# A two-layer decoder trunk in split fp32: the order of the opening, the first transfers, the last bank, and the gate sums

## The chip, the core and the metric

The kernel runs on one core of a Trainium2 chip. The core has a matrix engine (TensorE, here PE, with PEld for its weight loads), a vector engine (DVE), an activation engine (ACT), a general engine (POOL) and a queue engine that mainly issues DMA transfers (SP). Each runs its own instructions in order and waits on the others through semaphores. Sixteen DMA engines move data between HBM and the on-chip memory. Results of matmuls land in PSUM, which has eight banks of 128 x 512 fp32 values.

The metric is the time on the device of one execution, in microseconds (us); lower is better.

## The reference, cut to what matters

The input is 256 tokens of width 2048. Two layers run in turn, each a token mixer followed by an MLP with a squared ReLU of width 8192; each reads an RMS-normed stream and adds to it.

```python
def fox_attention(h, w_in, b_f, q_gain, k_gain, w_out):
    proj = h @ w_in                                   # q | k | v | forget gates
    q = rms_norm(q, q_gain); k = rms_norm(k, k_gain)  # per head of 128
    c = jnp.cumsum(jax.nn.log_sigmoid(f + b_f), axis=1)
    s = q @ k.T * scale + c_query - c_key             # causal
    return (softmax(s) @ v) @ w_out

def dilated_attention(h, w_in, q_gain, k_gain, w_out):
    # three groups of heads, dilations 1, 4, 16, ALiBi; one shared v;
    # the groups are merged by their softmax denominators
    return (num / den) @ w_out

for i in range(2):
    x = x + mixer_i(rms_norm(x, mix_norm_g[i]))
    h = rms_norm(x, mlp_norm_g[i])
    x = x + (relu(h @ w_up) ** 2) @ w_down
```

All weights are fp32, some 446 MB with the rest of what is read, and each weight is used once.

## The kernel before

**Split products.** Every fp32 operand of a large product is cut into a high part in the format that PE multiplies in one pass and a low part with the rest, and a product is three matmuls: high by high, high by low, low by high. A weight tile has 256 rows by 512 columns (512 KB). It is loaded as `raw` (five buffers), then `split` makes `wh` with a cast on ACT (L340) and `wl` with a subtraction on DVE (L341), five buffers each. `load` issues the transfers on SP's queue (L321); a `split` also issues the load of the tile four further on.

**A product.** `product_steps` goes through the 16 chunks of 128 input channels. One chunk is a step: two halves of the tokens by three matmuls of 512 columns (L375 to L377), six matmuls. Every second step ends one weight tile and splits another. The first layer's attention runs four rounds of three products (q, k, v); the forget gates are summed between the first q product and the first k product (`gate`, L706).

**Jobs and steps.** All work beside the products is written as generators. `jobs.tick()` runs after each step; a generator that yields a number sleeps for so many steps, one that yields a key sleeps until the key is done. So the program text puts the side work into a trace order between the matmuls. A scheduler then chooses the order of each engine's queue from that trace, unless edges forbid it. `pin` adds such edges: each traced instruction is tied behind the one before it on its engine. It is switched on at step 24. Ahead of it, and in places behind it, `behind(...)` ties single instructions behind others: casts, transposes, transfers, squares.

**The opening.** Eight transposes of the identity (`wake`, L146) run first. x comes in four tiles of 512 channels: `load_x(0)` issues the first one, half on SP and half on ACT's queue, then the first weight tile in the same way. The gain rows of the norm come on POOL's queue (`g_mix`, L158) and are turned on PE (L165). All later loads are held back by a one-element clear on DVE (L304) that is tied behind the copy of the turned gains (L166). `norm_chain` turns x for the first norm in eight pieces: four 128-column transposes into one bank (L518), scaled into a high part on ACT (L523) and a low part on DVE (L524). `more_constants` loads gate weights (`wf`, L191), gate bias and further gains after nine steps. The sums of squares (L534) run later, and the norm's factor is applied behind the first products.

**The end and the second layer's attention.** `last_product` is the last of the four products of the last MLP; it goes through three parts (tokens 0 to 127 whole, tokens 128 to 255 in two halves of 256 columns) with a bank for each, all three from the pool `ps_acc` of four banks, and each part is added up and stored as soon as it is done (L899, L901). The product before it holds two of the four banks until DVE has added them (L886). `dil_head` computes a head of the second layer: scores, softmax, a transposition through DRAM (`p_turned`), a split of the probabilities (`p_split`, ACT L669 and DVE L672), and after three more steps (two for the last pair of heads) the products with v (`pv`, L642 and L643, tile `po_d`).

Of the kernel before, what the change touches and what calls it, by code (L numbers as in the profile page):

```python
# [43 lines left out]
class Jobs:  # L44
# [5 lines left out]
    def __init__(self):  # L50
        self.now = 0
        self.live = []
        self.done = set()
        self.running = False
        self.each_step = lambda: None
# [37 lines left out]
def trunk(ctx: ExitStack, tc, x, fox_w_in, fox_b_f, fox_q_gain, fox_k_gain, fox_w_out, dil_w_in,  # L93
# [3 lines left out]
    pinned = {"last": None}  # L97
# [6 lines left out]
    def pin():  # L104
# [5 lines left out]
        if pinned["last"] is None:  # L110
            at = len(traced)
# [22 lines left out]
    nc.gpsimd.memset(warm, 0.0)  # L134
    nc.scalar.activation(warm, warm, AF.Exp)
# [6 lines left out]
    spare = ps_sc.tile([P, P], F32, tag="sc", name="spare")  # L142

    def wake(times):
        for _ in range(times):
            nc.tensor.transpose(spare, ident, ident)  # L146

    wake(8)
# [5 lines left out]
    def gain_rows(name, sources, queue=nc.sync):  # L154
        rows = work.tile([2 * KC, P], F32, tag="s", name=name, bufs=S_BUFS)
        at = 0
        for src in sources:
            queue.dma_start(rows[at:at + src.shape[0], :], src)  # L158
            at += src.shape[0]
        return rows[0:at, :]  # L160

    def gain_columns(name, rows, at):
# [3 lines left out]
        return nc.vector.tensor_copy(gain[:, at:at + n], ps[:, :n])  # L166

    per_chunk = "l (c p) -> (l c) p"
    mix_rows = gain_rows("g_mix", [mix_norm_g.rearrange(per_chunk, p=P)], nc.gpsimd)
# [17 lines left out]
    def more_constants():  # L187
        yield 9
        wf = work.tile([P, KC, FH], F32, tag="t2", name="wf")
        with behind(issued["load"]):  # L190
            nc.sync.dma_start(wf, fox_w_in[0][:, 3 * D:3 * D + FH].rearrange("(c p) n -> p c n", p=P))  # L191
            nc.sync.dma_start(bf, fox_b_f.to_broadcast([P, FH]))
            qk_rows = gain_rows("g_qk", [fox_q_gain, fox_k_gain, dil_q_gain[0], dil_k_gain[0]])
            mlp_rows = gain_rows("g_mlp", [mlp_norm_g.rearrange(per_chunk, p=P)])
        di = distances()
        yield 6
        with behind(*issued["n0"]):
            nc.scalar.copy(wfs[:, :, 0:FH], wf)
            nc.vector.tensor_sub(wfs[:, :, FH:2 * FH], wf, wfs[:, :, 0:FH].bitcast(F32))
# [88 lines left out]
    def behind(*instructions):  # L288
        stack = ExitStack()
        for i in instructions:  # L290
            stack.enter_context(tc.issue_after(getattr(i, "ins", i)))
        return stack

    def move(dst, src):

        with behind(issued["load"]):
            return nc.sync.dma_start(dst, src)
# [12 lines left out]
    def load():  # L310
# [6 lines left out]
        for c, width in cols:  # L317
            src = w[r:r + RAW_SUB * P, c:c + width].rearrange("(c p) n -> p c n", p=P)
            if i:
                with hold(t[:, 0, 0:1]):  # L320
                    issued["load"] = nc.sync.dma_start(t[:, :, at:at + width], src)  # L321
            else:

                for part, queue in enumerate((nc.sync, nc.scalar)):
                    queue.dma_start(t[:, part, at:at + width], src[:, part, :])
# [4 lines left out]
    def split():  # L330
        i = state["split"]
        per = RAW_SUB // W_SUB
        if i >= len(plan) * per:
            return
        raw = raws[i // per][:, (i % per) * W_SUB:(i % per + 1) * W_SUB, :]
        hi = wpool.tile([P, W_SUB, NC], F32R, tag="wh", name=f"wh{i}", bufs=W_BUFS)
        lo = wpool.tile([P, W_SUB, NC], F32R, tag="wl", name=f"wl{i}", bufs=W_BUFS)
        with behind(*([issued["gained"]] if i == 0 else issued.get("n0", []) if i < 2 * W_BUFS else [])):
            for part in ([slice(0, 1), slice(1, 2)] if i < 1 else [slice(0, W_SUB)]):
# [656 lines left out]
    with behind(issued["transposed"]):  # L996
        wake(3)
# [67 lines left out]
```

## Time and profile before

| | us |
|---|---|
| median of three runs | 2149.95 |
| lowest and highest run | 2149.67, 2149.97 |
| the profiled execution, its own time | 2150.94 |
| the profiled execution, span from first to last instruction | 2149.2 |
| PE busy in it | 2136.6 |
| DVE busy | 1425.8 |
| ACT busy | 1094.9 |
| POOL busy | 42.3 |

A row of the timeline has the start in us, the length in us, the engine, the line, the operation, the tile that is written `<-` those read, the shapes, and how many instructions are merged; in brackets the idle time of the engine before it and what ended it. PE's matmuls are pipelined: the row of one is longer than its share of the stream, so the pitch is read from start to start. A row of a stretch has its ends, its length, then busy time and number of instructions for PE, PEld, DVE, ACT and POOL (or for PE alone), the granted clock, the share of the DMA engines' time and GB/s. A row of waits has total time, number and the longest. "SPq" and "ACTq" are instructions that issue transfers.

### The profile page before, as it was taken

What the parts mean: (1) busy time and instruction counts of PE and PEld (TensorE: products, weight loads), DVE (VectorE), ACT (ScalarE), POOL (GpSimd) and SP (SyncE); (2) the same over time, 40 slices, a digit from 0 to 9 for tenths busy, and PEclk for the clock granted to TensorE, in tenths of its full rate; (3) what the DMA queues carried; (4) which work ended last, traced back from release to release, by engine and by line L of the source; (5) the groups of instructions that cost most, each with busy time, mean ns of one, the idle gap of its engine ahead of it and who ended that gap; (6) DMA issues with size and microseconds to landing.
All of it is one profiled execution on the core that took longest, in us unless ns stands there. A gap on an engine that the chain in (4) does not pass through costs nothing.

```text
span 2149.2 us, 29907 instructions
## 1 busy us (share of the span) xinstructions
PE 2136.6 (99%) x11120; PEld 1906.8 (89%) x11120; DVE 1425.8 (66%) x1893; ACT 1094.9 (51%) x1521; POOL 42.3 (2%) x40
## 2 busy tenths in 40 slices
PE   9999999999999999999999999999999999999998
PEld 7888888988998998998888888889988988988988
DVE  6788876785665565566668787667655655665664
ACT  6565655643443454455555655646544444444442
POOL 0000000000000000000010010000000000000000
PEclk9999999999999999999999999999999999999999
DMA  7888877766666656657777777768666566666663
GB/s 240 254 260 270 253 244 237 231 219 205 187 216 204 198 201 206 201 189 254 243 241 231 245 238 217 254 201 273 207 204 201 189 216 201 193 210 203 202 210 136
DMA packets 314531, 471.97 MB, mean 220 GB/s; under 512 B 36424, under 2 KB 124048, under 8 KB 314384
## 3 DMA queue, kind: packets, MB, share of 16 engines
q1 hardware_dynamic: 313792, 469.38, 68.2%
q8 instruction: 87, 1.43, 0.3%
q10 hardware_dynamic: 560, 0.66, 0.1%
q14 instruction: 60, 0.49, 0.1%
q0 software_dynamic: 32, 0.02, 0.0%
HBM read 446.35 MB, written 23.62 MB: 219 GB/s over the span
## 4 chain that ended last, share of the span: by engine, by line
PE 97%; DVE 1%; ACT 1%; DMA 1%; issue 0%; SPq 0%; POOL 0%; ACTq 0%; DVEq 0%; POOLq 0%
PE acc L375 21%; PE acc L376 21%; PE acc L377 21%; PE up_n1a_acc L440 5%; PE up_n3a_acc L440 5%; PE up_n3a_sc L440 3%; PE up_n1a_tp L440 3%; PE up_n1a_sc L440 3%; PE up_n3a_tp L440 3%; PE up_n1a_acc L444 3%; PE up_n3a_acc L444 3%; PE up_n3a_sc L444 1%; PE up_n3a_tp L444 1%; PE up_n1a_sc L444 1%; PE up_n1a_tp L444 1%; DVE wl L341 0%
## 5 line engine op out<-in xcount | busy, mean ns | idle before, releaser
L341 DVE TENSOR_TENSOR wl<-raw,wh 128x1024 fp32r<-128x1024 f32 (+1 forms) x801 | 970.1, 1221 | 636.9 <-ACT wh L340 624.7
L340 ACT CAST wh<-raw 128x1024 fp32r<-128x1024 f32 (+1 forms) x801 | 830.6, 1047 | 880.3 <-PE acc L377 580.0
L375 PE MATMUL acc<-wh,hT_n 128*128 128x512 f32 x896 | 343.1, 384 | 0.1
L376 PE MATMUL acc<-wl,hT_n 128*128 128x512 f32 x896 | 340.5, 380 | 0.1
L377 PE MATMUL acc<-wh,hT_n 128*128 128x512 f32 x896 | 340.3, 380 | 0.0
L376 PE MATMUL acc<-wl,aTh_n1a 128*128 128x512 f32 x512 | 194.2, 379 | 0.0
L377 PE MATMUL acc<-wh,aTl_n1a 128*128 128x512 f32 x512 | 194.2, 379 | 0.0
L375 PE MATMUL acc<-wh,aTh_n1a 128*128 128x512 f32 x512 | 194.2, 379 | 0.0
L377 PEld LDWEIGHTS acc<-wh,hT_n 128*128 128x128 f32 x896 | 169.9, 190 | 23.8
L375 PEld LDWEIGHTS acc<-wh,hT_n 128*128 128x128 f32 x896 | 170.0, 190 | 22.9 <-ACT wh L340 0.5
L376 PEld LDWEIGHTS acc<-wl,hT_n 128*128 128x128 f32 x896 | 170.2, 190 | 22.5 <-DVE wl L341 0.4
L376 PE MATMUL acc<-wl,aTh_n3a 128*128 128x512 f32 x480 | 182.1, 379 | 0.0
L377 PE MATMUL acc<-wh,aTl_n3a 128*128 128x512 f32 x480 | 182.1, 379 | 0.0
L375 PE MATMUL acc<-wh,aTh_n3a 128*128 128x512 f32 x480 | 182.1, 379 | 0.0
L440 PE MATMUL up_n1a_acc<-hT_n,wh 128*128 128x512 f32 x512 | 181.7, 382 | 0.0
L440 PE MATMUL up_n3a_acc<-hT_n,wh 128*128 128x512 f32 x512 | 181.6, 382 | 0.0
L444 PE MATMUL up_n3a_acc<-hT_n,wl 128*128 128x256 f32 x512 | 139.6, 273 | 0.0
L444 PE MATMUL up_n1a_acc<-hT_n,wl 128*128 128x256 f32 x512 | 139.6, 273 | 0.0
L376 PEld LDWEIGHTS acc<-wl,aTh_n1a 128*128 128x128 f32 x512 | 96.9, 189 | 13.7
L377 PEld LDWEIGHTS acc<-wh,aTl_n1a 128*128 128x128 f32 x512 | 96.9, 189 | 13.6
L440 PEld LDWEIGHTS up_n3a_acc<-hT_n,wh 128*128 128x128 f32 x512 | 97.0, 189 | 13.4
L375 PEld LDWEIGHTS acc<-wh,aTh_n1a 128*128 128x128 f32 x512 | 96.9, 189 | 13.4
(673 smaller groups left out, 3158.2 us busy)
## 6 DMA issues: line engine op xcount, KB each, us to landing
raw<-in_mlp_w_up_dram SPq DMA_DIRECT2D x256, 512.0 KB, 4.5
raw<-in_mlp_w_down_dram SPq DMA_DIRECT2D x256, 512.0 KB, 4.5
raw<-in_dil_w_in_dram SPq DMA_DIRECT2D x192, 256.0 KB, 3.3
raw<-in_fox_w_in_dram SPq DMA_DIRECT2D x95, 512.0 KB, 4.9
raw<-in_fox_w_out_dram SPq DMA_DIRECT2D x32, 512.0 KB, 4.5
raw<-in_dil_w_in_dram SPq DMA_DIRECT2D x32, 512.0 KB, 4.2
raw<-in_dil_w_out_dram SPq DMA_DIRECT2D x32, 512.0 KB, 3.8
blocks_n<-turned_n SPq DMA_DIRECT2D x96, 64.0 KB, 2.1
```

The source lines that it names most:

```text
L340: issued["cast"] = nc.scalar.copy(hi[:, part, :], raw[:, part, :])
L341: issued["cut"] = nc.vector.tensor_sub(lo[:, part, :], raw[:, part, :], hi[:, part, :].bitcast(F32))
L375: nc.tensor.matmul(acc[t], ah[:, tok], hi, start=first, stop=False)
L376: nc.tensor.matmul(acc[t], ah[:, tok], lo, start=False, stop=False)
L377: issued["product"] = nc.tensor.matmul(acc[t], al[:, tok], hi, start=False, stop=last)
L440: issued["product"] = nc.tensor.matmul(banks[b], hi[:, i, col], in_turn(tokens.rearrange("p x s -> p (x s)"), P // 2), start=first, stop=last)
L444: nc.tensor.matmul(banks[b][:, 0:S], lo[:, i, col], in_turn(tokens[:, 0, :], P // 2), start=False, stop=False)
```

## The change

- `pin` starts with the first instruction and is run at each step, and every `behind(...)` is taken out. The queues of all engines then follow the trace from the start.
- `wake` becomes a matmul of 512 columns with zeros that DVE clears, six ahead of everything and one behind the turned gains, in a bank of `ps_acc`.
- The first tile of x comes in three pieces (128, 128 and 256 channels), the gains behind the first of them, all on SP's queue; the first weight tile in two row blocks, the first on ACT's queue, the second on SP's. The seven loads behind the second weight tile are held back by a clear of the whole tile on POOL.
- The first three weight tiles are split by row blocks, and up to step 27 splits are placed by hand (`opening`) instead of one at each second step.
- The transposes of the first norm write each 256-column piece into a bank of its own (`ps_tp` and `ps_sc`) and come at other steps: x's tiles at 0, 3, 5 and 9 instead of 0, 2, 6 and 10, with two steps between the halves of the last two tiles. The squares of the first norm come a little later.
- `more_constants` issues its transfers after five steps instead of nine, and splits the gate weights one step earlier.
- `gate` sums high and low parts in one matmul of 512 columns, 16 instead of 32; DVE adds the two halves afterwards.
- `dil_head` waits four steps instead of three ahead of `pv` (but for the last pair).
- `last_product` takes its third bank from `ps_tp`.

```diff
-    nc.gpsimd.memset(warm, 0.0)
-    nc.scalar.activation(warm, warm, AF.Exp)
+    pinned["last"] = nc.gpsimd.memset(warm, 0.0).ins
+    jobs.each_step = pin
...
-    spare = ps_sc.tile([P, P], F32, tag="sc", name="spare")
+    spare = ps_acc.tile([P, NC], F32, tag="acc", name="spare")
+    zeros = work.tile([P, NC], F32R, tag="w", name="zeros", bufs=6)
+    nc.vector.memset(zeros.bitcast(F32), 0.0)
     def wake(times):
         for _ in range(times):
-            nc.tensor.transpose(spare, ident, ident)
-    wake(8)
+            nc.tensor.matmul(spare, zeros[:, 0:P], zeros, start=True, stop=True)
+    wake(6)
...
     def more_constants():
-        yield 9
+        yield 5
         wf = work.tile([P, KC, FH], F32, tag="t2", name="wf")
-        with behind(issued["load"]):
-            nc.sync.dma_start(wf, fox_w_in[0][:, 3 * D:3 * D + FH].rearrange("(c p) n -> p c n", p=P))
+        nc.sync.dma_start(wf, fox_w_in[0][:, 3 * D:3 * D + FH].rearrange("(c p) n -> p c n", p=P))
...
-        yield 6
-        with behind(*issued["n0"]):
-            nc.scalar.copy(wfs[:, :, 0:FH], wf)
+        yield 9
+        nc.scalar.copy(wfs[:, :, 0:FH], wf)
...
-    def hold(first):
-        if "held" not in issued:
-            return ExitStack()
-        with behind(issued["gained"]):
-            nc.vector.memset(first, 0.0)
-        return behind(*([issued["load"]] if issued["held"] == [] else []))
+    def hold(whole):
+        if "paced" in issued:
+            nc.gpsimd.memset(whole, 0.0)
...
+    def split_part(i, part):
+        raw, (hi, lo) = raws[i], splits[i]
+        nc.scalar.copy(hi[:, part, :], raw[:, part, :])
+        nc.vector.tensor_sub(lo[:, part, :], raw[:, part, :], hi[:, part, :].bitcast(F32))
...
             if i == W_SUB - 1:
                 used[0] += 1
-                split()
+                if "opening" not in issued:
+                    split()
...
-        acc = [ps_acc.tile([P, NC], F32, tag="acc", name=f"last{x}") for x in range(len(parts))]
+        acc = sums() + [ps_tp.tile([P, NC], F32, tag="tp", name="last")]
...
-                pt = ps_tp.tile([P, 2, S], F32, tag="tp", name=f"ptx_{tag}_{pr}")
...
+                for i, (pool, of) in enumerate(((ps_tp, "tp"), (ps_sc, "sc"))):
+                    pt = pool.tile([P, S], F32, tag=of, name=f"ptx_{tag}_{pr}_{i}")
...
-                yield 1
+                yield 1 if n < 2 else 2
...
-        pf = ps_sc.tile([2 * FH, S], F32, tag="sc", name="pf")
+        pf = ps_sc.tile([2 * FH, 2 * S], F32, tag="sc", name="pf")
         for k in range(KC):
-            for x, h in enumerate(lhs_h(tag)(k)):
-                nc.tensor.matmul(pf, wfs[:, k, :], h, start=k + x == 0, stop=k + x == KC)
+            both = hT[tag][k // 2][:, k % 2]
+            nc.tensor.matmul(pf, wfs[:, k, :], both.rearrange("p x s -> p (x s)"), start=k == 0, stop=k == KC - 1)
...
-        nc.vector.tensor_copy(f, pf)
+        nc.vector.tensor_copy(f, pf[:, 0:S])
+        nc.vector.tensor_add(f, f, pf[:, S:2 * S])
...
-        yield 2 if q4 == 3 else 3
+        yield 2 if q4 == 3 else 4
...
+    load_x(0, 0, P)
+    mix_rows = gain_rows("g_mix", [mix_norm_g.rearrange(per_chunk, p=P)])
+    load_x(0, P, 2 * P)
+    nc.sync.dma_start(first_raw[:, 1, :], first_w[:, 1, :])
+    load_x(0, 2 * P, NC)
...
+    load()
+    issued["paced"] = True
+    for what in (lambda: load_x(1), load, load, lambda: load_x(2), load):
+        what()
+    gain_columns("g_mix", mix_rows, 0)
+    wake(1)
+    row_blocks = [slice(i, i + 1) for i in range(W_SUB)]
+    split(())
+    split_part(0, row_blocks[0])
+    jobs.spawn(first(0))
+    split_part(0, row_blocks[1])
+    next_load()
+    load_x(3)
+    del issued["paced"]
+    issued["opening"] = True
+
+    def opening():
+        yield 1
+        split(row_blocks)
+        yield 2
+        split(row_blocks)
+        yield 1
+        split()
+        for _ in range(5):
+            yield 2
+            split()
+        yield 1
+        del issued["opening"]
         while state["split"] - used[0] < W_BUFS:
+            yield 4
             split()
```

More of the change, by code (lines that the diff above doesn't have):

```diff
@@ L318, in load @@
             src = w[r:r + RAW_SUB * P, c:c + width].rearrange("(c p) n -> p c n", p=P)
[L319 to L325, printed above, removed]
+            hold(t)
+            nc.sync.dma_start(t[:, :, at:at + width], src)
             at += width
@@ L969, in normed @@
         return lambda n: norm_chain(tag, col, n, ssp, wait(n), later(n))
[L972 to L980 removed]
+    first = normed("n0", 0, lambda n: (0, 3, 5, 9)[n], lambda n: (13, 12, 9, 7)[n])
@@ L989, in trunk @@
-    issued["gained"] = gained
-    issued["held"] = True
-    for what in (load, lambda: load_x(1), load, lambda: load_x(2), load, lambda: load_x(3), load):
-        what()
-        issued["held"] = []
-    del issued["held"]
-    jobs.spawn(first(0))
-    with behind(issued["transposed"]):
-        wake(3)
-    split()
     for n in range(1, NX):
         jobs.spawn(first(n))
-    jobs.spawn(rest())
+    jobs.spawn(opening())
     jobs.spawn(more_constants())
```

133 lines of the change are left out of this document (52 added, 81 removed).

## The prediction

> **What bounds the kernel now.** I read the page first: the span, the busy row, the chain of waits by engine.
>
> ```profile
> span 2149.2 us, 29907 instructions
> ...
> PE 2136.6 (99%) x11120; PEld 1906.8 (89%) x11120; DVE 1425.8 (66%) x1893; ACT 1094.9 (51%) x1521; POOL 42.3 (2%) x40
> ...
> PE 97%; DVE 1%; ACT 1%; DMA 1%; issue 0%; SPq 0%; POOL 0%; ACTq 0%; DVEq 0%; POOLq 0%
> ```
>
> TensorE (PE) is the bound. The change takes little work off it, so its worth lies in the 12.6 us in which PE is not busy and in products that run at a wrong pitch. The view of PE's waits says where the idle time is.
>
> ```profile
> PE spare L146 <- POOL ident masks.py:199: 2.5, 1, 2.5
> PE last L418 <- DVE x L886: 2.2, 1, 2.2
> PE po_d L642 <- DVE pTl_d L672: 1.9, 1, 1.9
> PE ps_g_mix L165 <- DMA g_mix<-in_mix_norm_g_dram: 1.8, 1, 1.8
> ...
> PE pf L706 <- DVE wfs L199: 0.2, 1, 0.2
> ```
>
> Each of the five is touched by the change. Next the timeline of the opening (start, length, engine, line, work).
>
> ```profile
> 0.84 0.20 POOL masks.py:197 MEMSET ident<- 128x128 f32 x1
> 0.98 0.10 POOL L139 MEMSET mhalf<- 128x8 f32 x1
> ...
> 2.53 1.97 PE L146 MATMUL spare<-ident 128*128 128x128 f32 x8 [2.53 <-POOL ident masks.py:199]
> ...
> 5.84 1.14 ACT L340 CAST wh<-raw 128x512 fp32r<-128x512 f32 x2 [3.09 <-DMA raw<-in_fox_w_in_dram]
> ...
> 6.34 0.31 PE L165 MATMUL ps_g_mix<-ident,g_mix 32*128 32x32 f32 x1 [1.84 <-DMA g_mix<-in_mix_norm_g_dram]
> ...
> 6.58 1.11 PE L518 MATMUL ptx_n<-ident,x 128*128 128x128 f32 x4
> ...
> 6.91 1.40 DVE L341 TENSOR_TENSOR wl<-raw,wh 128x512 fp32r<-128x512 f32 x2
> 6.93 0.38 SPq L321 DMA_DIRECT2D raw<-in_fox_w_in_dram  x1
> ...
> 7.74 0.47 ACT L523 ACTIVATE hT_n<-ptx_n,gain 128x256 fp32r<-128x256 f32 x1 [0.76 <-DVE wl L341]
> ...
> 8.24 0.48 DVE L524 SCALAR_TENSOR_TENSOR hT_n<-ptx_n,gain,hT_n 128x256 fp32r<-128x256 f32 x1
> ...
> 8.26 0.80 PE L375 MATMUL acc<-wh,hT_n 128*128 128x512 f32 x1
> ...
> 9.28 0.64 PE L375 MATMUL acc<-wh,hT_n 128*128 128x512 f32 x1
> ...
> 9.71 0.64 PE L376 MATMUL acc<-wl,hT_n 128*128 128x512 f32 x1
> ...
> 12.20 0.38 PE L376 MATMUL acc<-wl,hT_n 128*128 128x512 f32 x1
> 12.42 0.38 PE L377 MATMUL acc<-wh,hT_n 128*128 128x512 f32 x1
> ...
> 34.59 0.38 PE L377 MATMUL acc<-wh,hT_n 128*128 128x512 f32 x1
> ```
>
> The first product starts at 8.26. Products then follow each other every 0.43 us (9.28 to 9.71), and from 12.20 on every 0.216. The row at 34.59 is the 96th product, as many as the whole first projection has. The stretches of time, with the DMA share and GB/s last:
>
> ```profile
> 2.00:5.50 3.50, 1.97 (x8) 1.57 (x8) 0.00 (x0) 0.73 (x2) 1.02 (x5) 1.00 0.91 292
> 5.50:8.50 3.00, 2.16 (x9) 1.77 (x10) 1.81 (x11) 1.61 (x3) 0.46 (x2) 1.00 0.17 26
> 8.50:20.00 11.50, 11.28 (x48) 9.18 (x49) 6.84 (x11) 5.94 (x10) 0.00 (x0) 1.00 0.99 358
> ...
> 33.00:37.50 4.50, 4.50 (x23) 3.94 (x22) 2.66 (x4) 4.44 (x12) 0.00 (x0) 1.00 0.53 93
> ...
> 8.26:34.80 26.54, 26.32 (x125) 1.00 0.97 320
> ```
>
> From 5.5 to 8.5 us the DMA engines stand nearly empty: the later loads are queued behind the copy of the gain columns, whose 16 KB come last (6.34). So the opening is bound by the first loads and by this order.
>
> **Opening, the start.** Data flow from 2.0 us; the last byte of the first 1 MB (292 GB/s for 3.5 us) comes at 5.5 and the cast follows at 5.84, 0.34 later. Now the cast and the transposes wait for less: a quarter of x's first tile (128 KB), the gains (16 KB) and the first row block of the weights (256 KB). 400 KB at 292 GB/s end at 3.4, usable at 3.7; as x's pieces have rows a quarter as long I take 4.2. The cast then ends at 4.8 (half of 1.14). PE is the later: six wake products from about 1.3 us (the DVE clear of 512 columns isn't in the trace; between nothing and the 0.70 of a DVE subtraction of that size, I take 0.4) at 0.43 end at 3.9; the gain transpose waits for its load until 4.2 and takes 0.25; one more wake product 0.43; two transposes 0.43 and 0.1 to their end: 5.4. The activation takes 0.47 and the first product starts at **5.9**, 2.4 earlier. Upper bound: nothing lands before 5.84, cast and activation follow: 6.9. Lower bound: PE is at full pitch by then, 5.2.
>
> **Opening, after the start.** 96 products at 0.216 and 28 transposes at 0.107 (half of the 0.213 at which four take 1.11 while the pitch is doubled) are 23.7 us; before needs 26.54 and loses 2.8. Afterwards I allow 1.7: half of the first step's six products at double pitch (0.65); 0.5 at the third step, where the low half of the second weight tile stands on DVE behind two 0.48 scalings that wait for PE's transposes; 0.5 for the slower product behind each group of transposes, as before. The 96th product ends at 5.9+23.7+1.7 = 31.3, against 34.8: **3.5 us** gained. By the bounds 6.9 with all 2.8 gives 33.4, a gain of 1.4, and 5.2 with 0.5 gives 29.4, a gain of 5.4.
>
> On the doubled pitch, the Trainium skill ("TensorE: Matmul & The Clock Gate", Parts 1 and 4) says that the array's clock is halved until a window of about 3.4 us has been busy, and that transposes do not count as matmuls do. The trace agrees: the twelve transposes of the rows at 2.53 and 6.58 change nothing, and the pitch is halved within 4 us of products. By that rule the wake products could have the clock up at the first product, or a window late.
>
> **What I cost at nothing.** Seven POOL clears of 1024 columns now hold back the loads behind them on SP's queue. The trace has 0.20 us for 128 columns and 0.10 for 8, so 0.8 ns a column and 0.9 us each; bounds 0.2 (no slope) and 1.6 (all slope). Even at 1.6 the last ends near 14 us; x's last tile is first needed at the ninth step, near 21. The sixth waits for the release of the first weight tile (about 8 us); behind it are the clear and load of x's last tile. The loads of the gate weights and gains, with their 64-byte rows (the stretch 33.0 to 37.5: 93 GB/s), move ahead of the tenth weight tile on SP. Ahead of them lie 6.9 MB, 19 us at 358 GB/s: the hole comes near 21 and the tenth tile lands near 27; it is needed at 37. Without that cover it would cost 4.5. From step 24 on the order was that of the program text already, so the dropped order constraints there change nothing. The sum of squares comes one step later; its cover is the third projection's start 11 steps on. Splits run only two or three tiles ahead of PE until step 27, and ACT has eleven casts in the last 24 us of that:
>
> ```profile
> L340 ACT CAST wh<-raw 128x1024 fp32r<-128x1024 f32 (+1 forms) x801 | 830.6, 1047 | 880.3 <-PE acc L377 580.0
> ```
>
> At 1.05 that is 11.5 us; the sums of squares kept ACT busy for 4.44 of 4.50 us from 33.0 on, without a wait of PE. Two tiles ahead are a cover of 5.2 us; without it each late cast would cost up to its 1.05.
>
> **Gate.**
>
> ```profile
> 37.61 0.38 PE L376 MATMUL acc<-wl,hT_n 128*128 128x512 f32 x1
> ...
> 37.75 0.42 DVE L199 TENSOR_TENSOR wfs<-wf,wfs 128x256 fp32r<-128x256 f32 x1
> ...
> 38.23 0.91 PE L706 MATMUL pf<-hT_n,wfs 128*32 128x256 f32 x6 [0.24 <-DVE wfs L199]
> ...
> 39.22 3.21 PE L706 MATMUL pf<-hT_n,wfs 128*32 128x256 f32 x26
> ```
>
> 32 matmuls at 0.12 (3.21 over 26) are 3.84 us; 16 of 512 columns at 0.216 are 3.45: 0.4 gained. The step from 37.61 to 38.23 is 0.4 too long for want of the gate weights, whose split now comes one step earlier in the order and some 1.3 us ahead of PE: 0.4 more, between 0 and 0.4. One more DVE addition (at most the 0.42 of the row) lies in the gate's chain, three steps ahead of PE's next use. Together **0.8**.
>
> **The value products of the second layer.**
>
> ```profile
> 1358.38 0.27 PE L642 MATMUL po_d<-pTh_d,dv2h 128*128 128x256 f32 x1
> 1360.06 0.41 DVE L672 TENSOR_TENSOR pTl_d<-turned_d,pTh_d 128x256 fp32r<-128x256 f32 x1
> 1360.53 0.38 PE L642 MATMUL po_d<-pTl_d,dv2h 128*128 128x256 f32 x1 [1.88 <-DVE pTl_d L672]
> ```
>
> The group moves one step later: six products, 1.3 us. DVE reaches the low half at the same time, so PE waits 0.75 instead of 2.04: **1.3**, at least 0 (the group feeds only the output projection, and nothing queued behind it on PE needs it), at most all 2.1.
>
> **The last product.**
>
> ```profile
> 2123.03 0.28 PE L420 MATMUL last<-wh,aTl_n3a 128*128 128x256 f32 x1
> 2124.58 1.40 DVE L886 SCALAR_TENSOR_TENSOR x<-acc,rstd_n,x 128x512 f32<-128x512 f32 x2
> 2125.47 0.35 PE L418 MATMUL last<-wh,aTh_n3a 128*128 128x256 f32 x1 [2.17 <-DVE x L886]
> ```
>
> PE waits until DVE has added up the previous product, whose bank the third part takes. The transposition pool's bank was last used by the up projection four products earlier, so the wait of 2.44-0.11 goes: **2.3**. Next late would be the weights split on DVE, two tiles ahead there.
>
> **Sum.** 3.5+0.8+1.3+2.3 = 7.9 us. The profiled execution took 2150.94 (1.7 around its span), which leaves 2143.0; the median of the runs, 2149.95, is 1.0 lower, so I forecast **2142.0**.
>
> **Rivals.** *Transfers bind the opening:* with the DMA share at 0.91 and then 0.99 the earlier start brings nothing by the 96th product. For it stand these shares, against it the empty 5.5 to 8.5. Time 2142.0+3.5 = 2145.5; 0.20. *Full pitch at once:* the wake products end the doubled pitch before the first product, as four us of products ended it at 12.2; 0.65 and two transposes' 0.2 go: 2141.1; 0.20. (The skill's clock rule above allows it if its window falls well.) *The free bank frees nothing:* PE stops at the same place for the split weights of DVE, which also has the late addition ahead of it: 2144.3; against it, the next split is four steps off; 0.08. *Slower: the POOL clears.* If 1024 columns take 5 us (the page calls POOL spans rough), the seventh ends at 36 instead of 8 to 14, x's last tile is usable 3 us later (2 for the load, 1 for transposes and scaling), and the 13th step, due at 25.7 (5.9, twelve steps of 1.3, six groups of transposes of 0.5, 1.2 lost), starts at 39: 13 us lost, 2155. It turns slower than before when a clear takes over 4.2 us, since then it eats all 7.9; against it stand 0.20 and 0.10; 0.04. [...]
>
> **The numbers.** The forecast has 0.48. A change of 0.2% (4.3 us) is about what a measurement here tells from none, so faster means under 2145.65: the forecast, full pitch, the bank (0.76) and two fifths of the transfer case (0.08) make 0.84; the rest of it 0.12 for the same; 0.04 slower. The bounds of the parts (1.4 or 5.4 for the opening, 0.4 or 0.8, 0 or 2.1, 2.3) add up to 4.1 and 10.6, 2145.9 to 2139.3; with most of the transfer case 2139.0 to 2146.5, which leaves 0.15 outside.
>
> **What would show it.** First product near 5.9 and the 96th ended near 31.3; no DMA hole at 5.5 to 8.5; the rows of waits for `last` and `pf` gone, that for `po_d` near 0.7; 16 gate matmuls 0.216 apart; the tail from the last matmul on unchanged. I am wrong if new waits of PE for `wh`, `wl` or `x` appear in the first 60 us, if POOL's clears take several us, or if another `po_d` group waits.

## The result, and the profile after

| | us |
|---|---|
| kernel before, median of 8 runs beside those of the changed one (lowest, highest) | 2150.27 (2149.67, 2151.75) |
| changed kernel, median of 8 runs (lowest, highest) | 2144.37 (2142.77, 2145.01) |
| ratio, with its 95% interval | 0.9970 (0.9959 to 0.9981) |
| changed kernel, the profiled execution | 2142.78 |

The change saves 5.9 us. The forecast was 2142.0, so the measured median lies 2.4 above it, inside the range. The profiled execution lies at the low end of the eight runs, which matters below.

The head of the page and the view of PE's waits, changed kernel:

```profile
span 2141.1 us, 29878 instructions
...
PE 2134.4 (100%) x11100; PEld 1900.5 (89%) x11100; DVE 1427.9 (67%) x1890; ACT 1094.9 (51%) x1523; POOL 49.8 (2%) x46
```

```profile
PE spare L146 <- DVE zeros L142: 1.5, 1, 1.5
PE ps_g_mix L165 <- DMA g_mix<-in_mix_norm_g_dram: 0.8, 1, 0.8
PE acc L363 <- ACT hT_n L506: 0.3, 1, 0.3
...
PE acc L364 <- DVE wl L329: 0.2, 1, 0.2
```

The rows for `last`, `po_d` and `pf` are gone. What is left is the opening (and a wait of 0.3 at `sc_f`, as before), and two waits there are new: the scaling of the first transposes (`hT_n`) and the low half of a weight tile (`wl`). The timeline of the changed kernel, from the opening, the gate and one group of value products (lines have moved: L363 to L365 are the products, L504 the transposes, L328 the cast, L683 the gate, L621 and L622 the value products, L407 to L409 the last product):

```profile
1.39 0.95 POOL L293 MEMSET x<- 128x1024 f32 x1
...
5.29 0.21 PE L165 MATMUL ps_g_mix<-ident,g_mix 32*128 32x32 f32 x1 [0.85 <-DMA g_mix<-in_mix_norm_g_dram]
...
6.71 0.48 PE L363 MATMUL acc<-wh,hT_n 128*128 128x512 f32 x1 [0.35 <-ACT hT_n L506]
...
9.72 0.38 PE L365 MATMUL acc<-wh,hT_n 128*128 128x512 f32 x1
...
10.18 0.48 PE L363 MATMUL acc<-wh,hT_n 128*128 128x512 f32 x1
...
10.90 0.48 PE L364 MATMUL acc<-wl,hT_n 128*128 128x512 f32 x1 [0.24 <-DVE wl L329]
...
31.95 0.38 PE L365 MATMUL acc<-wh,hT_n 128*128 128x512 f32 x1
...
32.44 3.87 PE L683 MATMUL pf<-hT_n,wfs 128*32 128x512 f32 x16
36.14 0.38 PE L363 MATMUL acc<-wh,hT_n 128*128 128x512 f32 x1
...
1354.44 0.41 DVE L649 TENSOR_TENSOR pTl_d<-turned_d,pTh_d 128x256 fp32r<-128x256 f32 x1
...
1356.09 0.27 PE L621 MATMUL po_d<-pTh_d,dv2h 128*128 128x256 f32 x1
1356.20 0.28 PE L621 MATMUL po_d<-pTl_d,dv2h 128*128 128x256 f32 x1
```

The first product starts at 6.71 (before 8.26), the 96th at 31.95 (before 34.59). The third step's first product comes 0.46 behind the one ahead of it (9.72 to 10.18) and the next 0.72 later (10.18 to 10.90) instead of 0.216: the second weight tile's cast started only at 9.50. The chain of waits of the opening has it:

```profile
3.24 6.25 DMA raw<-in_fox_w_in_dram
...
9.50 0.63 ACT wh L328
```

The tile's transfer was issued at 3.24 and landed at 9.48. The stretches, changed kernel, columns as in the prediction's:

```profile
2.00:5.50 3.50, 2.65 (x8) 1.53 (x7) 0.00 (x0) 1.38 (x3) 3.50 (x5) 1.00 0.85 227
5.50:8.50 3.00, 2.65 (x15) 1.97 (x15) 2.36 (x5) 1.37 (x3) 0.56 (x2) 1.00 0.94 287
8.50:20.00 11.50, 11.18 (x59) 9.07 (x58) 8.54 (x15) 8.03 (x17) 2.16 (x4) 1.00 1.05 391
```

The hole from 5.5 to 8.5 is filled (share 0.94, before 0.17), but from 2.0 to 5.5 the same engines move 227 GB/s, where before they moved 292.

### The profile page after: what moved, and what is told of

The parts are those of the page before. It is cut to its first block, busy times and chain, and to the rows that moved or that the text cites. A ratio compares the mean times of both kernels' runs of the same rounds, so it can differ in the third digit from the quotient of the medians.

```text
span 2141.1 us, 29878 instructions
## 1 busy us (share of the span) xinstructions
PE 2134.4 (100%) x11100; PEld 1900.5 (89%) x11100; DVE 1427.9 (67%) x1890; ACT 1094.9 (51%) x1523; POOL 49.8 (2%) x46
## 3 DMA queue, kind: packets, MB, share of 16 engines
q8 instruction: 87, 1.43, 0.3%
## 4 chain that ended last, share of the span: by engine, by line
PE 99%; ACT 0%; DMA 0%; issue 0%; SPq 0%; DVE 0%; ACTq 0%
PE acc L364 21%; PE acc L363 21%; PE acc L365 21%; PE up_n3a_acc L429 5%; PE up_n1a_acc L429 5%; PE up_n3a_sc L429 3%; PE up_n3a_tp L429 3%; PE up_n1a_sc L429 3%; PE up_n1a_tp L429 3%; PE up_n1a_acc L433 3%; PE up_n3a_acc L433 3%; PE up_n1a_tp L433 1%; PE up_n1a_sc L433 1%; PE up_n3a_tp L433 1%; PE up_n3a_sc L433 1%; PE sc_d L672 0%
## 5 line engine op out<-in xcount | busy, mean ns | idle before, releaser
L328 ACT CAST wh<-raw 128x1024 fp32r<-128x1024 f32 (+1 forms) x803 | 830.5, 1044 | 863.5 <-PE acc L365 556.9
L363 PE MATMUL acc<-wh,hT_n 128*128 128x512 f32 x896 | 342.8, 383 | 0.4 <-ACT hT_n L506 0.3
L365 PE MATMUL acc<-wh,hT_n 128*128 128x512 f32 x896 | 339.7, 379 | 0.0
L363 PE MATMUL acc<-wh,aTh_n1a 128*128 128x512 f32 x512 | 194.0, 379 | 0.0
L365 PE MATMUL acc<-wh,aTl_n1a 128*128 128x512 f32 x512 | 194.0, 379 | 0.0
L365 PEld LDWEIGHTS acc<-wh,hT_n 128*128 128x128 f32 x896 | 169.3, 189 | 24.2 <-DVE hT_n L507 0.2
L363 PEld LDWEIGHTS acc<-wh,hT_n 128*128 128x128 f32 x896 | 169.5, 189 | 23.4 <-ACT hT_n L506 0.6
L363 PE MATMUL acc<-wh,aTh_n3a 128*128 128x512 f32 x480 | 181.9, 379 | 0.0
L365 PE MATMUL acc<-wh,aTl_n3a 128*128 128x512 f32 x480 | 181.9, 379 | 0.0
L365 PEld LDWEIGHTS acc<-wh,aTl_n1a 128*128 128x128 f32 x512 | 96.8, 189 | 13.8
L363 PEld LDWEIGHTS acc<-wh,aTh_n1a 128*128 128x128 f32 x512 | 96.8, 189 | 13.6
L429 PEld LDWEIGHTS up_n1a_acc<-hT_n,wh 128*128 128x128 f32 x512 | 96.8, 189 | 13.5
```

Of the source, the lines that this page charges most:

```text
L328: nc.scalar.copy(hi[:, part, :], raw[:, part, :])
L363: nc.tensor.matmul(acc[t], ah[:, tok], hi, start=first, stop=False)
L365: nc.tensor.matmul(acc[t], al[:, tok], hi, start=False, stop=last)
L429: nc.tensor.matmul(banks[b], hi[:, i, col], in_turn(tokens.rearrange("p x s -> p (x s)"), P // 2), start=first, stop=last)
```

## The experiments

**Theories.** The changed kernel's runs fall into two groups, some near 2142.8 and most at 2144.2 to 2145.1 (one lies between, at 2143.77). Theory A: the groups differ by when PE leaves the doubled pitch. Theory B: they differ by transfers that land late, far behind an opening that is always the same. The late three parts (gate, `po_d`, `last`) are measured by putting them back or doing them alone. An edit stands as a diff against the changed kernel, where nothing else is said.

**The changed kernel once more** (no edit).

> The changed kernel once more, for a second profile and for the spread of its runs (2142.77 to 2145.01 so far, the profiled one 2142.78). Theory A, the clock: in some executions the doubled pitch of PE lasts into the first products, so a run near 2144.5 shows products 0.43 us apart behind the first one, and past 40 us the same work as in the trace at hand. Theory B, late landings: the opening is the same in every execution (first product 6.7, 96th product 32.0), and a run near 2144.5 has a wait of PE of 1 to 2 us far behind it, at tiles that go through DRAM (fkT, pTl). Both expect the same times, 2142.7 to 2145.1.

Median 2144.72 of 7 runs (2142.87 to 2145.08); the profiled execution took 2144.51. Its timeline:

```profile
8.07 0.63 PE L365 MATMUL acc<-wh,hT_n 128*128 128x512 f32 x1
...
8.49 0.63 PE L363 MATMUL acc<-wh,hT_n 128*128 128x512 f32 x1
...
10.70 0.38 PE L364 MATMUL acc<-wl,hT_n 128*128 128x512 f32 x1
...
10.91 0.38 PE L365 MATMUL acc<-wh,hT_n 128*128 128x512 f32 x1
...
33.62 0.38 PE L365 MATMUL acc<-wh,hT_n 128*128 128x512 f32 x1
```

The whole first step runs at 0.43 (8.07 to 8.49) and the pitch is halved only in the second (10.70 to 10.91); in the first trace it was halved before the first product. The 96th product starts 1.67 later, and the execution took 1.73 longer. This is theory A. Nearly all of the difference lies ahead of the 96th product, so theory B is out for these two; nor did the gains, which the start waits for, come later: they were turned at 5.05 there, against 5.29 in the first trace.

**More wake products, and none.**

```diff
-    wake(6)
+    wake(8)
```

> The changed kernel with eight instead of six products with zeros ahead of everything, so that PE is busy until the gains land near 5.2 us. Theory A: the pitch is halved ahead of the first product in more executions; the median falls from 2144.4 to 2143 or less and the spread to under 1.2 us. Theory B: median and spread as without (within 0.4 us), since PE only fills a wait for the gains.

Median 2144.72 of 6 runs (2143.12 to 2145.16): no change, where theory A expected 2143 or less. So two more products do not halve the pitch earlier in most executions. The profiled execution (2143.12) has the full pitch early, and one other run (2143.23) lies beside it. Its third step waits for the cast of the second weight tile:

```profile
10.50 0.48 PE L363 MATMUL acc<-wh,hT_n 128*128 128x512 f32 x1 [0.39 <-ACT wh L328]
```

```diff
-    wake(6)
+    wake(0)
```

> The changed kernel without the six first products with zeros (the one behind the gains stays). Both theories expect the doubled pitch in the first products in every execution, for about 3.4 us. Theory A: that is what the slow executions already have, so the median rises only to 2144.5 to 2145.5, and the spread falls under 1 us. Theory B: it comes on top of everything, the median rises by 1.3 to 1.9, to 2145.7 to 2146.3, with the spread of 2 us as before.

Median 2144.79 of 7 runs (2143.88 to 2145.35), so six wake products bring the median nothing. What they may buy is the minority of executions near 2142.8, 3 of the changed kernel's 15 and none of these 7. The median is as theory A expected; the spread, 1.5, lies between the two expectations. In the profiled execution the pitch stayed doubled until 11.9.

**The late three parts alone.** The kernel before, with the bank, the gate sums in 512 columns and the four steps, and its own opening:

```diff
-        acc = [ps_acc.tile([P, NC], F32, tag="acc", name=f"last{x}") for x in range(len(parts))]
+        acc = sums() + [ps_tp.tile([P, NC], F32, tag="tp", name="last")]
...
+            nc.tensor.matmul(pf, wfs[:, k, :], both.rearrange("p x s -> p (x s)"), start=k == 0, stop=k == KC - 1)
...
-        yield 2 if q4 == 3 else 3
+        yield 2 if q4 == 3 else 4
```

> The kernel before with three parts of the change alone, all behind the opening: the free bank for the last product, gate sums of 512 columns, and four steps ahead of the value products. My sum: 2.3 + 0.4 + 1.3 = 4.0 us off the kernel before, near 2146.3, and the opening with the gate's wait (3.9) is the rest. Rival: the wait at po_d is no fixed thing and only the bank and the gate count, 2.7 us off, near 2147.6. Rival: the opening brings little because its transfers bind, and these three bring nearly all, near 2144.6.

Median 2146.04 of 11 runs (2145.57 to 2146.54), ratio to the kernel before 0.9981 (0.9972 to 0.9990); the kernel before had 2150.02 beside it. So these parts bring 4.0. What the opening adds in the median is 2146.04 - 2144.72 = 1.3. How the 4.0 is made up is not as the forecast had it, since the gate sums bring nothing. First this kernel's gate, then the product behind the gate in the kernel before:

```profile
37.22 0.38 PE L376 MATMUL acc<-wl,hT_n 128*128 128x512 f32 x1
37.84 0.89 PE L706 MATMUL pf<-hT_n,wfs 128*32 128x512 f32 x3 [0.24 <-DVE wfs L199]
...
38.81 3.21 PE L706 MATMUL pf<-hT_n,wfs 128*32 128x512 f32 x13
...
42.13 0.48 PE L377 MATMUL acc<-wh,hT_n 128*128 128x512 f32 x1
```

```profile
42.53 0.48 PE L377 MATMUL acc<-wh,hT_n 128*128 128x512 f32 x1
```

13 matmuls of 512 columns take 3.21 us, as the 26 of 256 columns in the prediction's rows did. From the product ahead of the gate to the one behind it pass 4.91 us (37.22 to 42.13), before 4.92 (37.61 to 42.53), and the wait for the gate weights is still there.

**Three steps ahead of the value products.**

```diff
-        yield 2 if q4 == 3 else 4
+        yield 2 if q4 == 3 else 3
```

> The changed kernel with three steps ahead of the value products of the second layer instead of four. My step: the fourth step took 1.3 us of a wait away, so PE waits at po_d again by about that in most executions, the median rises by 1.2 from 2144.6 to 2145.8, and the runs spread over more than 2.5 us. Rival: the wait came from a transfer that landed late in the execution that was shown; in the traces of the changed kernel the low half is ready 1.2 us ahead of PE, so with three steps it waits for 0.1 or not at all, and the median stays within 0.4 of 2144.6.

Median 2145.45 of 11 runs (2143.98 to 2146.66), 0.7 above the changed kernel: half-way between the two expectations, with the spread of the first (2.7). The view of the tile `po_d`, here first:

```profile
L622 PE MATMUL po_d<-turned_d,dv3w x8: 275/276/276, 1427.7 to 1441.1; 128*128 128x128 f32 x8
...
L621 PE MATMUL po_d<-pTl_d,dv1h x4: 275/276/378, 1256.2 to 1271.2; 128*128 128x256 f32 x4
...
  DVE pTl_d L649: 1.2, 4
```

and of the changed kernel:

```profile
L622 PE MATMUL po_d<-turned_d,dv3w x8: 275/275/275, 1425.6 to 1439.1; 128*128 128x128 f32 x8
```

A matmul of 378 ns is one that began behind a wait (the others take 275): with three steps several groups wait a little for the low half, with four none does. The group's last matmul comes 2.0 later (1441.1 against 1439.1), of which 1.04 had been lost in the opening (the 96th product at 32.99 against 31.95): 0.96 for these waits.

**The last bank as before.**

```diff
-        acc = sums() + [ps_tp.tile([P, NC], F32, tag="tp", name="last")]
+        acc = [ps_acc.tile([P, NC], F32, tag="acc", name=f"last{x}") for x in range(len(parts))]
```

> The changed kernel with the third bank of the last product taken from the same pool as before. My step: the wait for the addition of the previous product comes back with 2.2 us idle before the last product's third part, 2.3 in all, median 2146.9. Rival, part of it was hidden elsewhere (DVE's last work sets the end): under 1.5, below 2146.1.

Median 2147.24 of 10 runs (2144.94 to 2148.32), 2.5 above the changed kernel, so the wait of 2.3 is back and the rival is out. The timeline shows the wait and something behind it:

```profile
2117.52 0.28 PE L409 MATMUL last<-wh,aTl_n3a 128*128 128x256 f32 x1
...
2119.96 0.35 PE L407 MATMUL last<-wh,aTh_n3a 128*128 128x256 f32 x1 [2.17 <-DVE x L862]
...
2122.30 0.63 PE L407 MATMUL last<-wh,aTh_n3a 128*128 128x512 f32 x1
...
2122.73 0.63 PE L408 MATMUL last<-wl,aTh_n3a 128*128 128x512 f32 x1
```

and a stretch of this kernel, of PE alone:

```profile
2121.00:2124.50 3.50, 3.50 (x15) 0.51 0.32 118
```

About 1.1 us after PE resumes, its granted clock falls to 0.51 for 3.4 us, and products of 512 columns come 0.43 apart (2122.30 to 2122.73). The wait costs 2.33 (2.44 - 0.11), the dip half of 3.4, 1.7. Over the whole span the dip shows in the mean clock, which each run lists: 0.999 here, 1.000 in the changed kernel's trace. The kernel before ran 64 times beside the experiments: 29 runs list 0.999 and have a median of 2151.72, 35 list 1.000 and have 2150.14. This kernel has 0.999 in 6 of 10 runs. The changed kernel and those variants of it, or of its late parts, in which PE never waits some 2 us between products have it in none of 73. So with the free bank the changed kernel also escapes a dip of the clock, and the kernel before seems to suffer one, of 1.6 us, in a little under half of its executions. Where the clock fell is known from this trace alone: neither trace of the kernel before has the dip, and behind its wait of 2.17 at `last` the clock reads 1.00. In that kernel the wait at `po_d` could be the place as well.

**The gains first.**

```diff
-    load_x(0, 0, P)
     mix_rows = gain_rows("g_mix", [mix_norm_g.rearrange(per_chunk, p=P)])
+    load_x(0, 0, P)
     load_x(0, P, 2 * P)
```

> The changed kernel with the gains issued ahead of x's first quarter instead of behind it. Theory C, place in the queue: the gains land near 3.5 instead of 5.1, PE comes to the transposes when x's first quarter lands, and the first product starts near 6.0 instead of 6.7 to 7.0; as the pitch is halved at a time of its own, an execution with the late halving gains only half of that, so the median goes to 2144.2 and the fastest to 2142.2. Theory D, a copy of 16 KB takes some 4 us wherever it stands: they land at 4.7, the first product starts 0.3 earlier at most, and nothing is seen in the median.

Median 2143.66 of 5 runs (2143.36 to 2144.24), 1.1 below the changed kernel by the medians; the intervals of the ratios to the kernel before overlap (0.9955 to 0.9980 against 0.9959 to 0.9982). The gains' row in the view of transfers, here and then in the changed kernel (the last number is us from issue to landing):

```profile
g_mix<-in_mix_norm_g_dram SPq DMA_DIRECT2D x1, 16.0 KB, 2.6
```

```profile
g_mix<-in_mix_norm_g_dram SPq DMA_DIRECT2D x1, 16.0 KB, 3.9
```

So theory D, some 4 us wherever it stands, is out. In the changed kernel the gains are issued at 1.28 behind 128 KB of x and land near 5.2. Here they are there when the wake products end:

```profile
4.37 0.31 PE L165 MATMUL ps_g_mix<-ident,g_mix 32*128 32x32 f32 x1
...
6.40 0.80 PE L363 MATMUL acc<-wh,hT_n 128*128 128x512 f32 x1
```

The pitch is still doubled in this execution until 11; against the likewise late one of the changed kernel the 96th product (33.03) comes 0.59 earlier and the time, 2143.89, is 0.62 shorter.

**x's first tile in one transfer**, on top of that:

```diff
-    load_x(0, P, 2 * P)
+    load_x(0)
     nc.sync.dma_start(first_raw[:, 1, :], first_w[:, 1, :])
-    load_x(0, 2 * P, NC)
```

> As the one before, with x's first tile in one transfer of 2 KB rows instead of three of 512 bytes to 1 KB rows. Theory E, small rows cost transfer rate: the 231 to 302 GB/s between 4 and 8 us rise to some 340, the second weight tile lands by 8.2 instead of 9.5, the wait of PE for it at the third step goes, the first product still starts by 6.8, and the median is 0.5 below that of the kernel before it in this list. Rival, smaller pieces let PE start early: the first product waits for the whole 512 KB, to 7.3 or later, and the median is 0.4 or more above.

Median 2144.76 of 8 runs (2143.33 to 2144.87), 1.1 worse than with pieces. The stretch after 5.5 in the kernel that this one edits, then two stretches of this one, and PE's rows:

```profile
5.50:8.50 3.00, 2.86 (x9) 2.10 (x8) 1.62 (x4) 1.52 (x3) 0.39 (x1) 1.00 0.94 332
```

```profile
2.00:5.50 3.50, 3.37 (x8) 1.80 (x7) 0.78 (x2) 1.36 (x3) 3.50 (x5) 1.00 0.90 229
5.50:8.50 3.00, 1.80 (x9) 1.29 (x10) 1.18 (x4) 1.34 (x3) 0.40 (x1) 1.00 1.01 370
```

```profile
6.35 0.66 PE L504 MATMUL ptx_n<-ident,x 128*128 128x128 f32 x4 [0.98 <-DMA x<-in_x_dram]
7.36 0.48 PE L363 MATMUL acc<-wh,hT_n 128*128 128x512 f32 x1 [0.35 <-ACT hT_n L506]
```

From 5.5 to 8.5 whole rows of 2 KB move faster (370 GB/s against 332), but from 2.0 to 5.5 they move 229, about the 227 of the changed kernel's pieces. So short rows do not explain the low rate of the first stretch; its cause stays open. The first product comes 1 us later, and the start counts for more.

**One wake product behind the first transposes**, on top of the gains first:

```diff
     split_part(0, row_blocks[0])
     jobs.spawn(first(0))
+    wake(1)
     split_part(0, row_blocks[1])
```

> The gains ahead of x's first quarter, as in mix_first, and one more product with zeros behind the first four transposes, where PE idles for 0.35 us ahead of the first product. If only the missing share of products in a window keeps the pitch doubled (theory A), more executions have it halved early, and the median falls from 2143.7 to 2143.0 or less, the fastest to 2142.2. If transposes, which stay in the way, are what counts against it, the median stays within 0.4 of 2143.7.

> The mix_wake version once more, beside w_early. If its five runs were no luck of the clock (all within 2142.98 to 2143.49), the median is again 2143.0 to 2143.5 with no run near 2144.7. If the extra product only happened to meet a good phase, runs at 2144 and above appear, as 11 of 15 runs of the changed kernel are.

Medians 2143.28 (2142.98 to 2143.49) and 2143.53 (2142.55 to 2143.55) of 5 runs each, ratios to the kernel before 0.9961 (0.9947 to 0.9975) and 0.9965 (0.9952 to 0.9978). No run lies near 2144.7. This is the best version of the study, 0.8 to 1.4 below the changed kernel by the medians (the intervals of the ratios overlap), with a spread of 1.0 against 2.2. How much of it is the added product is not shown: with the gains first alone the median is 0.1 to 0.4 higher, and the five runs there spread by only 0.9. In its first trace the full pitch is there before the first product:

```profile
5.89 0.48 PE L363 MATMUL acc<-wh,hT_n 128*128 128x512 f32 x1
...
10.50 0.48 PE L363 MATMUL acc<-wh,hT_n 128*128 128x512 f32 x1 [0.96 <-ACT wh L328]
```

The first product comes where the prediction had put it, at 5.89, 0.82 ahead of the changed kernel's; the third step begins at 10.50, 0.32 behind it. PE has only moved its wait to the second weight tile.

**That tile ahead of x's third piece**, on top of the last version:

```diff
-    load_x(0, 2 * P, NC)
     raws.append(first_raw)
     state["raw"] += 1
     load()
+    load_x(0, 2 * P, NC)
```

> The mix_wake version with the second weight tile's transfer issued ahead of the third piece of x. Theory 'the second weight tile binds': in the traces whose pitch is full early the third step begins at 10.18 to 10.66 whatever the start of the first product (5.89 to 7.36), and the 96th product starts 21.8 later. If it is the place in the queue that makes the tile late, 256 KB less ahead of it at 281 GB/s bring it 0.9 earlier: the third step near 9.6, the 96th product near 31.4, time near 2142.3. Theory 'the rate binds, not the order': x's third piece now lands behind 512 KB, up to 1.9 later; PE then waits at the second step's transposes (from 7.58 on) for x, 0.5 to 1.3, and the third step begins no earlier than 10.2: the 96th product at 32.0 to 32.8, time 2142.9 to 2143.7.

Median 2144.42 of 8 runs (2143.99 to 2145.91), 1 us worse than without the edit. PE's wait:

```profile
9.90 0.66 PE L504 MATMUL ptx_n<-ident,x 128*128 128x128 f32 x4 [1.84 <-DMA x<-in_x_dram]
```

Now x's third piece is what is late. The chain of waits has it in flight from 3.56 on, as long as the weight tile was:

```profile
3.56 6.30 DMA x<-in_x_dram
```

and the stretch with the landing ahead of it:

```profile
5.50:8.50 3.00, 2.56 (x11) 1.66 (x9) 1.62 (x4) 1.41 (x3) 0.83 (x2) 1.00 0.71 222
```

So the place in the queue is no cure: whichever of the two stands last lands at 9.5 to 10.2. Theory "the rate binds, not the order" expected that wait, at most 1.3 of it, and a time of 2142.9 to 2143.7; the wait is longer and the time worse. The engines' mean share is only 0.71 here, so their joint rate does not explain all of it; why this transfer takes 6.3 us stays open.

**The kernel before, once more** (no edit).

> The kernel before once more, for a second trace; its runs spread from 2148.4 to 2153.7, those of late3 only by 1 us. My account: the two waits of 2.0 to 2.4 us at po_d and last are there or not much smaller in each execution, and behind one of them the granted clock falls to a half for about 3.4 us in some, 1.6 us more. An execution above 2151 then shows such a stretch; one near 2150 shows the two waits alone. Rival: the spread lies in the opening, and the first product or the 96th is over 1 us off 8.3 and 34.6.

2149.78, against 2150.94 in the trace that the prediction used. Its timeline:

```profile
33.97 0.38 PE L377 MATMUL acc<-wh,hT_n 128*128 128x512 f32 x1
...
1357.79 0.27 PE L642 MATMUL po_d<-pTh_d,dv2h 128*128 128x256 f32 x1
1359.33 0.38 PE L642 MATMUL po_d<-pTl_d,dv2h 128*128 128x256 f32 x1 [1.26 <-DVE pTl_d L672]
```

The 96th product is 0.62 earlier than in that trace and the pitch at `po_d` 0.61 shorter (1.54 against 2.15). Together they are 1.23, the whole difference of 1.16 between the two executions. The rival asked for more than 1 us in the opening; about half of the difference lies there.

**The traces side by side.** Start of the first product, of the third step and of the 96th product, and the profiled execution's time, for the kernels that have all three late parts and the new opening:

| kernel | first product | third step | 96th product | time | time less 96th |
|---|---|---|---|---|---|
| changed | 6.71 | 10.18 | 31.95 | 2142.78 | 2110.83 |
| wake(8) | 6.72 | 10.50 | 32.27 | 2143.12 | 2110.85 |
| gains first and one wake product | 5.89 | 10.50 | 32.27 | 2143.13 | 2110.86 |
| x whole | 7.36 | 10.66 | 32.44 | 2143.33 | 2110.89 |
| gains first and one wake product, again | 6.29 | 10.89 | 32.67 | 2143.53 | 2110.86 |
| second weight tile ahead of x's third piece | 6.40 | 11.78 | 33.55 | 2144.41 | 2110.86 |
| gains first | 6.40 | late pitch | 33.03 | 2143.89 | 2110.86 |
| changed, again | 7.05 | late pitch | 33.62 | 2144.51 | 2110.89 |
| wake(0) | 7.88 | late pitch | 34.50 | 2145.35 | 2110.85 |

The last column is the same within 0.06 us in all nine traces: whatever these kernels differ by happens ahead of the 96th product. In the first five the third step begins between 10.18 and 10.89 while the first product moves by 1.5, and the 96th product follows 21.8 later in each. In three of them (wake(8) and both with one wake product) ACT waits for the second weight tile, which lands at 9.8 to 10.2; in the changed kernel it lands at 9.48, just as ACT comes free. With x whole it is ACT that is late, since it scales x until 10. So once the pitch is full early, an earlier start brings nothing, because the second weight tile lands too late for it; the floor is near 2142.8 (the lowest run of all has 2142.55).

## Why the prediction was right, and where it was not

**The last product** was right: 2.3 forecast, 2.33 in the traces, and no split of DVE took the wait's place. The dip of the clock behind the wait was not in the forecast, since the trace of before had none.

**The gate** came out near its number, 0.73 against 0.8, by luck. From the product ahead of it to the one behind it the kernel before took 4.92, the changed one 4.19 (31.95 to 36.14). The step that failed is "16 of 512 columns at 0.216 are 3.45": the late three parts alone show that these 16 take as long as the 32 did, so that 0.4 is nothing. (The 0.12 for the matmuls before came from a row's length, which holds the whole of its last matmul, and the 0.216 is the pitch of the large products.) What is real is the wait for the gate weights, 0.4 as forecast. The remaining 0.3 is the transposition of the q and k gains, which stands inside the gate before (39.06) and ahead of the 96th product in the changed kernel (30.61), where it costs about as much again.

**The value products** were mis-sized by the step that DVE "reaches the low half at the same time". In the changed kernel the low half ends 1.2 ahead of the group (1354.44 + 0.41 against 1356.09), so nothing of the 0.75 is left and the whole 2.04 went in that pair of traces. With three steps in the changed kernel the waits are worth 0.7 to 1.0 only. The wait depends on the execution (2.04 and 1.43 in the two traces of before), so 1.3 was a fair middle and no more. Gate, value products and bank together were forecast at 0.4 + 1.3 + 2.3 = 4.0 without the late gate weights, and measured 4.0. That too is luck in part: the gate brought nothing and the value products less, and a share of the dip, which was not in the forecast, makes up for them.

**What was costed at nothing** did cost nothing. A clear took 0.95 (0.9 forecast); the rival that POOL makes it slower is out. The view of PE's waits has none for a weight or for x between the 96th product and the end.

**The opening** is where the forecast failed: 3.5, and 0.4 for the gate's wait, against 1.3 in the median. Three steps of it went wrong.

1. "I take 4.2" for the landings. The first row block of the weights was cast at 4.45, but the gains, which stood behind x's first piece, landed near 5.2, and the start waits for them. The version with the gains first shows that it was the place in the queue: there they land at 3.4. It is worth 1.1 in the median. The rate of 292 GB/s did not hold either (227), and short rows do not explain that, as the 229 of the version with x whole show. The first product came at 6.71, 0.8 late, near the upper bound of 6.9.
2. "half of the first step's six products at double pitch (0.65)". In 11 of 15 runs the time fits a pitch that stays doubled through the whole first step and the transposes behind it (2144.2 and above), as in the second trace; that costs 1.7 against the early case. The rival *full pitch at once* (0.20) is the profiled execution and the minority: by the times it came in 3 of 15 runs. From the first product to the end of the 96th that execution took 25.5, as the forecast's 25.4, but not for the forecast's reasons: none of the 0.65 for the doubled pitch was lost there, and other losses took its place, 0.75 of them at the third step.
3. "the median of the runs, 2149.95, is 1.0 lower" than the profiled execution. The second trace of before shows that this 1.0 lay in the opening and in `po_d`, which the change takes out, so it was counted twice. Without it the forecast is 2143.0.

The rival *transfers bind the opening* (0.20) is half right: the start did bring something, but with an early pitch the second weight tile, due at the third step, costs 0.75 (0.46 + 0.72 less twice 0.216). The forecast took 0.5 there, for a low half that stands late on DVE, and not for a tile that lands late. In these traces, starts earlier than 6.7 are eaten there. The empty stretch from 5.5 to 8.5 that spoke against it held less than it seemed, since the engines moved 227 and 287 GB/s in the opening's first two stretches and not the 358 that the kernel before moved from 8.5 on. In the profiled execution the errors cancel, which is luck: 2.64 for the opening, 0.73, 2.04 and 2.33 are 7.7 of the 8.2 saved (7.9 forecast); some 0.4 is not placed.

## What to carry to other kernels

Sum a forecast against one execution, and do not shift it by that execution's distance from the median when the change removes the very places where executions differ. Take the pitch of small matmuls from start to start and for their own shape; 16 of 512 columns cost here what 32 of 256 did. Do not carry a rate from one arrangement of transfers to another (292 GB/s became 214 to 254 in the same stretch), and put the 16 KB that everything waits for ahead of the first large piece. In an opening bound by loads, moving one load forward only pays until the next one is due, so write down for each load the time at which it is needed.

## What the hardware showed that was not expected

A wait of PE of about 2.2 us can halve its clock afterwards, in some executions. In the one trace that shows it the dip began 1.1 us behind the wait and lasted 3.4 us; in both traces of before nothing follows the same wait. The version with the second tile early waits 1.8 at x's third piece and has one run of eight with a mean clock of 0.999, at 2145.91, 1.5 above its median. The Trainium skill ("TensorE: Matmul & The Clock Gate", HAM oscillation) puts the harmful gap at over 3.4 us; here 2.2 was enough, so the measurement decides. One reading, not shown: what counts is how busy a whole window of 3.4 us was, and the one that ended at 2121.0 held the wait.

The time at which the opening's pitch is halved differs between executions of one kernel (before the first product, or at 10.4) and between versions (at 8.9 with three steps ahead of the value products, at 11.9 without wake products), so the six wake products, 2.9 us, catch it in few. With the gains first PE had products of 512 columns from 1.52 to 5.2 and again from 6.40, and the pitch was halved only at 11, so the first 3.7 us of products were not enough there. The Trainium skill ("TensorE: Matmul & The Clock Gate", Part 1) calls the window free-running and the transition variable for that reason; these traces agree that it varies. One product more, behind the transposes, went with a narrow spread of 1 us in ten runs, but the gains first without it spread by 0.9 in five, and its own second trace has the full pitch only from about 5.7.

In these stretches of the opening the granted clock reads 1.00 while the pitch is doubled (as in the 332 GB/s row of the gains-first kernel, whose products come 0.43 apart until 11); only the dip near the end reads 0.51. At the start the pitch has to be read from start to start.
